# A layer of a hybrid streaming encoder on one core: its program is ordered by another timing model

## The chip, the core and the metric

The kernel runs on one core of a Trainium2 chip (trn2). The metric is the device time of one execution in microseconds (us), the median of several runs; less is better. The engines are called PE (TensorE, the matmuls), PEld (its weight loads), DVE (VectorE), ACT (ScalarE), POOL (GpSimd) and SP (SyncE, which here issues every DMA).

## The reference, cut to what matters

One layer is computed for a prompt of 2048 tokens and a sample of 32 tokens, all in float32, with model width 1024:

```python
def layer(x):                                   # for the prompt and for the sample
    z = rms_norm(x, norm1) @ w_in               # 3592 columns: 7 streams of 512, and 8 forget logits
    o_a = hgrn2(q, f, i)                        # 4 heads, state 128x128, chunks of 64 tokens, in order
    o_a = rms_norm_head(o_a) * silu(g)
    o_b = softmax(q k / 8 + sums of log f) v    # 8 heads of 64, causal, q and k RMS-normed
    x = x + concat(o_a, o_b) @ w_out
    return x + square(relu(rms_norm(x, norm2) @ w_up)) @ w_down     # 4096 hidden columns
```

Keys, values, forget logits and the recurrent states are outputs too.

## The kernel before, in words

**Tiling.** The prompt is cut into four quarters of 512 tokens, numbered 0 to 3; quarter 2 also carries the 32 tokens of the sample (544 columns, done as twice 272). Each float32 operand is split into a high and a low part in fp32r, and each product is made of three matmuls (`mm3`, lines 174 to 181, through the helper `mm`, line 100: high by high, high by low, low by high). So a tile of a projection, 1024 rows deep, is 24 matmuls of 128x128 by 512 columns that accumulate in one PSUM tile of the tag `mm`, of which there are two before the feed-forward part and three in it.

**Weights.** `load_w` (lines 158 to 171) brings a block of 512 KB through SP into `wr`, makes its high part on ACT (`wh`, line 163) and its low part on POOL in four instructions of 256 columns (`wl`, line 169). Each of the three has two buffers.

**POOL's other work.** The norms of rows (`build`, lines 222 to 264) add their sums and raise them to the power -0.5 on POOL (`rs`, lines 249, 155 and 156); DVE multiplies the row by that (`row`, line 251), PE transposes it (`ta`, line 104), and ACT and DVE make `ahi` and `alo` of it (lines 201 and 202). The norms along partitions (`squares`, lines 286 to 295) make a square and its low part on POOL (`t`, lines 290 and 294), which PE sums (`tk`, `tq`, `th`).

**Side work and main work.** The main work, called dense, is the projections: `fox` (the attention's streams), `heads` (the recurrent part's streams), `out_proj` and `ffn`. Beside it run generators of small steps: the recurrent part's tails (`xa`, `th`, `xu`, four times `xo`, with the state `S` on DVE, line 717), and the attention (`st`, `ot`, `mx`, `mt`, `rs`), whose PSUM tiles of the tag `x` are three in all. Small results of the tails live in twelve buffers of the tag `t`.

**What sets the order.** The program is written out by one Python function. The class `Flow` (lines 41 to 72) keeps a clock of its own that each matmul moves on by its estimated time; a side step that yields a latency is due that much later on this clock, and `dense` lets all due steps in after every three matmuls:

```python
    def dense(self, *gens):
        for g in gens:
            for _ in g:
                self.pump()
```

The latencies are constants (line 88: 5.0, 8.0, 7.0 and 4.5; line 90 paces the attention). What `Flow` writes is the program's order, and an instruction's place in it is its priority. After that the tile library's context plays the whole program on a timing model: whenever the model finds an engine free, the first instruction in priority whose inputs and buffers the model has ready is put next on that engine. The outcome is one fixed list for each engine and for SP's queue, with semaphore waits. On the chip each engine goes through its list in order and waits where the list is too early. The stages at the end of the function follow each other as

```python
    flow.dense(fox(A, (0,)))                       # quarter 0, then 1
    flow.dense(heads((0, 1), (0, 1)), heads((0,), (2, 3)))
    flow.dense(heads((1,), (2, 3)))                # then fox for 2 and 3, and heads((2, 3), ...)
    tmp_stack.close(); ps_stack.close()            # buffers of the first half end here
    flow.dense(out_proj(0), out_proj(1)); ffn(0); ffn(1) with out_proj(2); ffn(2) with out_proj(3); ffn(3)
```

(shortened; the last two lines stand in lines 1327 to 1361). `build(2)` writes the activations of quarter 2 over those of quarter 0, so it ends after the last projection of quarter 0, and `fox` of quarter 2 needs it.

Of the kernel before, what the change touches and what calls it, by code (L numbers as in the profile page):

```python
# [71 lines left out]
                self.pump()  # L72


@with_exitstack
def hymba_step(
    ctx: ExitStack,
    tc: tile.TileContext,
    x_prompt, x_sample, cache_k, cache_v, cache_logf, state_hgrn,
# [1316 lines left out]
```

## Time and profile before

| | |
|---|---|
| median of 3 runs | 2918.09 us (2916.07 to 2918.6) |
| profiled execution | 2912.88 us, of it 2911.2 us from the first to the last instruction |
| mean granted TensorE clock | 0.996 |
| busy: PE, PEld, DVE, ACT, POOL | 2847.8, 2423.8, 1680.2, 1386.3, 1278.7 us |

The busy time of an engine is the union of its instructions' records. The profiled execution is 5.2 us shorter than the median of the runs, and 1.7 us of it lie outside the span of instructions.

### The profile page before, as it was taken

Reading aid. Unit: us, or ns where it says so; the run is one execution under the profiler, and the core shown is the slowest. Engines: PE = TensorE matmul, PEld = TensorE weight load, DVE = VectorE, ACT = ScalarE, POOL = GpSimd, SP = SyncE. Lnnn points to the kernel's source line nnn. Section 1 sums busy time; section 2 is a strip of 40 time slices with the busy share of each in tenths; the row PEclk is TensorE's granted clock in tenths of the full one; section 3 lists DMA queues with packets and bytes.
Section 4 is the critical chain, followed back from the end, with each engine's and each line's share of the span. In section 5 each row is a group of like instructions: output and inputs, shape, how many; then the busy total and the mean of one; then the engine's idle time right before and its main releaser. Section 6 shows DMA issues by size and latency. Waiting matters only on the chain.

```text
span 2911.2 us, 43685 instructions
## 1 busy us (share of the span) xinstructions
PE 2847.8 (98%) x15568; PEld 2423.8 (83%) x15568; DVE 1680.2 (58%) x3283; ACT 1386.3 (48%) x2447; POOL 1278.7 (44%) x1744
## 2 busy tenths in 40 slices
PE   7999999999999999999999999999999999999999
PEld 5787877988789778888888888978999989988887
DVE  6336677656666677666565555465665554443333
ACT  5555676777555545444444444444444433222222
POOL 5653344453223444444444444434333454455554
PEclk9999999999999999999999999999999999999999
DMA  6762444776324563434347344444533333243333
GB/s 180 211 170 86 122 137 127 208 193 175 87 80 116 168 227 106 123 107 122 111 123 228 117 120 116 129 134 117 180 113 102 92 109 95 87 131 105 94 94 102
DMA packets 463658, 381.91 MB, mean 131 GB/s; under 512 B 34432, under 2 KB 363408, under 8 KB 463440
## 3 DMA queue, kind: packets, MB, share of 16 engines
q1 hardware_dynamic: 463440, 379.12, 44.9%
q8 instruction: 123, 2.02, 0.3%
q14 instruction: 95, 0.78, 0.1%
HBM read 316.63 MB, written 62.40 MB: 130 GB/s over the span
## 4 chain that ended last, share of the span: by engine, by line
PE 64%; DVE 1%; ACT 0%; DMA 0%; POOL 0%; issue 0%; SPq 0%; DVEq 0%; ACTq 0%; POOLq 0%
PE mm L100 55%; PE st L100 3%; PE ot L100 3%; PE mx L100 1%; PE ta L104 0%; DMA row<-X 0%; PE rs L100 0%; DMA acc<-in_x_prompt_dram 0%; PE tx L104 0%; PE ty L104 0%; POOL wl L169 0%; DVE acc L882 0%; PE mt L104 0%; DVE pl L878 0%; ACT wh L163 0%
## 5 line engine op out<-in xcount | busy, mean ns | idle before, releaser
L169 POOL TENSOR_TENSOR wl<-wr,wh 128x256 fp32r<-128x256 f32 x1536 | 1121.2, 761 | 1500.3 <-ACT wh L163 1354.6
L100 PE MATMUL mm<-ahi,wh 128*128 128x512 f32 (+1 forms) x2528 | 895.9, 354 | 2.4 <-DVE acc L1056 1.3
L100 PE MATMUL mm<-alo,wh 128*128 128x512 f32 (+1 forms) x2528 | 881.7, 349 | 0.0
L100 PE MATMUL mm<-ahi,wl 128*128 128x512 f32 (+1 forms) x2528 | 881.2, 349 | 0.0
L163 ACT CAST wh<-wr 128x1024 fp32r<-128x1024 f32 x384 | 403.3, 1050 | 749.5 <-PE mm L100 668.4
L100 PEld LDWEIGHTS mm<-ahi,wh 128*128 128x128 f32 x2528 | 478.2, 189 | 62.3 <-DVE t L628 1.7
L100 PEld LDWEIGHTS mm<-ahi,wl 128*128 128x128 f32 x2528 | 477.2, 189 | 59.2 <-issue 0.5
L100 PEld LDWEIGHTS mm<-alo,wh 128*128 128x128 f32 x2528 | 478.4, 189 | 56.3
L1056 DVE TENSOR_TENSOR acc<-acc,mm 128x512 f32<-128x512 f32 x480 | 326.5, 685 | 161.5 <-PE mm L100 159.0
L874 ACT ACTIVATE st<-st 128x512 f32<-128x512 f32 (+1 forms) x320 | 169.3, 529 | 332.9 <-PE st L100 189.0
L878 DVE TENSOR_TENSOR pl<-st,ph 128x512 fp32r<-128x512 f32 (+1 forms) x320 | 198.5, 620 | 204.3 <-ACT ph L876 203.3
L100 PE MATMUL mm<-wh,uh 128*128 128x512 f32 x768 | 306.9, 400 | 1.3 <-ACT uh L1117 0.8
L100 PE MATMUL mm<-wh,ul 128*128 128x512 f32 x768 | 302.9, 395 | 0.0
L100 PE MATMUL mm<-wl,uh 128*128 128x512 f32 x768 | 302.8, 394 | 0.0
L1116 DVE TENSOR_TENSOR mm<-mm,r 128x512 f32<-128x512 f32 (+1 forms) x160 | 95.9, 599 | 300.6 <-ACT r L1115 299.0
L100 PEld LDWEIGHTS mm<-wh,uh 128*128 128x128 f32 x768 | 144.6, 188 | 39.3 <-DVE acc L1056 5.5
L100 PEld LDWEIGHTS mm<-wh,ul 128*128 128x128 f32 x768 | 144.9, 189 | 35.0 <-DVE ul L1118 0.2
L882 DVE TENSOR_TENSOR acc<-acc,st 128x512 f32<-128x512 f32 (+2 forms) x288 | 173.5, 602 | 0.0
L876 ACT CAST ph<-st 128x512 fp32r<-128x512 f32 (+1 forms) x320 | 169.9, 532 | 7.4
L100 PEld LDWEIGHTS mm<-wl,uh 128*128 128x128 f32 x768 | 145.0, 189 | 30.8
L834 DVE TENSOR_REDUCE mc<-mx 128x1 f32<-128x512 f32 x192 | 130.6, 686 | 41.2 <-PE mx L100 40.6
L100 PE MATMUL mm<-uh,wh 128*128 128x272 f32 x512 | 149.5, 292 | 0.2 <-DVE acc L1149 0.2
(293 smaller groups left out, 4177.6 us busy)
## 6 DMA issues: line engine op xcount, KB each, us to landing
wr<-in_w_up_dram SPq DMA_DIRECT2D x128, 512.0 KB
wr<-in_w_down_dram SPq DMA_DIRECT2D x128, 512.0 KB
wr<-in_w_in_dram SPq DMA_DIRECT2D x96, 512.0 KB
kB<-KS SPq DMA_DIRECT2D x160, 128.0 KB
kA<-KS SPq DMA_DIRECT2D x80, 256.0 KB
V<-VS SPq DMA_DIRECT2D x80, 256.0 KB
wr<-in_w_out_dram SPq DMA_DIRECT2D x32, 512.0 KB
out_dram<-t SPq DMA_DIRECT2D x32, 256.0 KB
```

What stands on the lines that cost most here:

```text
L100: pe.matmul(out, lhsT, rhs, start=start, stop=stop)
L163: act.copy(hi, raw)
L169: pool.tensor_tensor(fl(lo)[:, s], fl(raw)[:, s], fl(hi.bitcast(F32))[:, s], op=ALU.subtract)
L834: dve.tensor_reduce(out=mc[:, j, kb:kb + 1], in_=mx[:, 0:n], axis=AX.X, op=ALU.max)
L874: act.activation(st[:, off:], st[:, off:], AF.Exp)
L876: act.copy(ph[:, off:], st[:, off:])
L878: dve.tensor_tensor(pl[:, off:], st[:, off:], ph.bitcast(F32)[:, off:], op=ALU.subtract)
L882: dve.tensor_tensor(acc[:, off:], acc[:, off:], st[:, off:], op=ALU.add)
L1056: dve.tensor_tensor(acc[:, t, c], acc[:, t, c], ps, op=ALU.add)
L1116: dve.tensor_tensor(z, z, r, op=ALU.mult)
```

## The change

The function is renamed `hymba_body` and keeps its text. A new `hymba_step` is called in its place. It opens a critical section of the outer context, in which the outer context doesn't order instructions, and inside it a second tile context on the same core, made with `schedule_with_timeline_sim=True`. The body is written into that second context, with the same `Flow`, constants, tiles and buffers. The second context orders it as described above, but plays it on the library's more detailed timing model (sequencers with queues of issued instructions, the tails of writes, the time a semaphore takes, the PE clock, fixed costs of POOL's instructions, which by the library's own description the plain model leaves out) in place of the plain one.

```diff
+def hymba_step(outer: tile.TileContext, *args):
+
+    with outer.tile_critical(), tile.TileContext(outer.nc, schedule_with_timeline_sim=True) as tc:
+        hymba_body(tc, *args)
+
+
 @with_exitstack
-def hymba_step(
+def hymba_body(
     ctx: ExitStack,
     tc: tile.TileContext,
     x_prompt, x_sample, cache_k, cache_v, cache_logf, state_hgrn,
```

## Rows read from the trace of the kernel before

**Rows 1.** The page's first part: busy time, share of the span and instructions

```profile
PE 2847.8 (98%) x15568; PEld 2423.8 (83%) x15568; DVE 1680.2 (58%) x3283; ACT 1386.3 (48%) x2447; POOL 1278.7 (44%) x1744
```

**Rows 2.** Busy time by stage: window, length, busy and count per engine, clock, DMA

```profile
0.00:25.00 25.00, 8.22 (x37) 5.93 (x38) 21.40 (x55) 15.87 (x36) 10.99 (x29) 1.00 0.74 206
25.00:200.00 175.00, 168.55 (x781) 135.11 (x779) 57.12 (x99) 100.81 (x180) 118.52 (x148) 0.98 0.71 195
200.00:430.00 230.00, 220.78 (x1272) 183.28 (x1271) 160.75 (x366) 145.05 (x270) 81.39 (x99) 1.00 0.40 112
430.00:520.00 90.00, 82.23 (x525) 71.07 (x526) 67.99 (x151) 60.65 (x131) 40.09 (x51) 0.96 0.50 145
520.00:660.00 140.00, 140.00 (x847) 123.62 (x846) 86.68 (x185) 99.71 (x202) 74.10 (x87) 1.00 0.71 196
660.00:1000.00 340.00, 332.01 (x2124) 281.98 (x2124) 227.16 (x506) 200.72 (x414) 110.28 (x128) 0.99 0.44 124
1000.00:1040.00 40.00, 36.46 (x163) 27.47 (x162) 31.04 (x61) 22.13 (x41) 10.38 (x14) 1.00 0.72 246
1040.00:1800.00 760.00, 758.68 (x3395) 621.43 (x3394) 473.65 (x822) 332.96 (x528) 334.44 (x477) 1.00 0.45 131
1800.00:1960.00 160.00, 155.17 (x886) 134.25 (x885) 88.95 (x154) 73.21 (x132) 65.90 (x99) 0.99 0.45 130
1960.00:2560.00 600.00, 599.32 (x4040) 560.45 (x4039) 333.24 (x691) 238.25 (x398) 261.30 (x374) 1.00 0.38 112
2560.00:2911.00 351.00, 346.35 (x1514) 279.22 (x1512) 132.18 (x203) 96.91 (x120) 171.35 (x243) 1.00 0.36 105
```

**Rows 3.** Timeline of PE around 991: start, length, instruction, idle and releaser

```profile
987.28 0.40 PE L100 MATMUL th<-t,oner 128*128 128x512 f32 x1
991.00 0.50 PE L100 MATMUL th<-t,oner 128*128 128x512 f32 x1 [3.32 <-POOL t L294]
991.34 0.40 PE L100 MATMUL mm<-ahi,wh 128*128 128x512 f32 x1
...
992.47 0.63 PE L100 MATMUL mm<-alo,wh 128*128 128x512 f32 x1
992.89 0.63 PE L100 MATMUL mm<-ahi,wl 128*128 128x512 f32 x1
```

**Rows 4.** Timeline of POOL before the same wait

```profile
986.55 3.18 POOL L169 TENSOR_TENSOR wl<-wr,wh 128x256 fp32r<-128x256 f32 x3
989.69 1.26 POOL L294 TENSOR_TENSOR t<-t,t 128x512 fp32r<-128x512 f32 x1
```

**Rows 5.** Timeline of PE, then DVE, then POOL, around 447

```profile
447.12 0.58 PE L104 MATMUL mt<-identr,mpad 128*2 128x128 f32 x4 [4.16 <-DVE t L756]
...
444.72 1.28 DVE L251 SCALAR_TENSOR_TENSOR row<-row,rs,gbc 128x1024 f32<-128x1024 f32 x1 [2.82 <-POOL rs L156]
...
440.80 2.83 POOL L169 TENSOR_TENSOR wl<-wr,wh 128x256 fp32r<-128x256 f32 x4 [5.18 <-ACT wh L163]
```

**Rows 6.** Who waited for whom, all engines: total us, times, longest

```profile
DVE row L251 <- POOL rs L156: 49.2, 17, 7.9
```

**Rows 7.** Chain that ended last, in order of time: start, us, what

```profile
1034.74 26.15 PE mm L100 x114
...
2335.39 56.97 PE mm L100 x297
```

**Rows 8.** Timeline of the start and of the end

```profile
0.78 1.28 ACT L142 ACT_TABLE_LOAD   x1 [0.78 <-PEq L1383]
...
2907.19 0.69 DVE L1056 TENSOR_TENSOR acc<-acc,mm 128x512 f32<-128x512 f32 x1 [0.71 <-PE mm L100]
```

**Rows 9.** SP's queue around the attention's end

```profile
2338.55 0.34 SPq L923 DMA_DIRECT2D MTH<-mh  x1
...
2341.81 0.37 SPq L274 DMA_DIRECT2D ahi<-MTH  x1
```

## The prediction

> **What bounds the kernel now.** I read the page's busy line first. PE is busy for 2847.8 of 2911.2 us, the next engine for 58% of the span [rows 1]. So no other engine's throughput matters, and a change of order alone can only act on what PE loses: the time in which it stands idle, and the time in which its clock is low. The table by stage says where that is [rows 2]. Idle time of PE is length less busy time: 16.8 us in the first 25, then 6.5, 9.2, 7.8, 0.0, 8.0 and 3.5 us in the stages up to 1040, 1.3 us from 1040 to 1800, 4.8 us from 1800 to 1960, 0.7 us from 1960 to 2560, and 4.7 us in the last stage: 63.2 us in all. The feed-forward part is closed. The 39.8 us of the stages 25 to 1040 and 1800 to 1960 are what an order could win, for there the small steps of the side work stand between the dense matmuls, and dense matmuls stand behind each wait.
>
> The timelines show what such a wait is. At 987.28 PE does the first of two sums over squares and then idles 3.32 us for POOL's `t`, although a dense matmul that waited for nothing comes right behind, at 991.34 [rows 3]. POOL was late because three pieces of a weight's low part, 3.18 us, lay before the 1.26 us that PE needed [rows 4]. The list had put the sum there because the model that made it had POOL done by then. At 447 it is the same one step removed: POOL does four pieces of a weight (2.83 us) before a row's `rs`, DVE's `row` waits 2.82 us for that, the DVE instructions behind it wait with it, one of them releases PE, and PE has lost 4.16 us [rows 5]. DVE waits for this `rs` 17 times, 49.2 us in total [rows 6]. These waits are errors about POOL's time, in lists that are otherwise good.
>
> After the wait at 991 the matmuls start 0.42 us apart (992.47, 992.89) [rows 3], where 114 matmuls of the same width in a closed stretch took 26.15 us, 0.229 each [rows 7]. That is the lower of the clock's two levels, 1.2 against 2.4 GHz, and PE had idled 3.3 us before it fell. By stage the granted clock is 0.98, 0.96, 0.99 and 0.99 in the stages from 25, 430, 660 and 1800 [rows 2]. At half speed half of the time is lost, so one minus the mean clock is the share lost: 175 x 0.02 + 90 x 0.04 + 340 x 0.01 + 160 x 0.01 = 12.1 us, with two digits of clock behind it.
>
> **The change part by part.** Instructions are neither added nor taken away in the body: the three matmuls of each product, POOL's pieces and every DMA stay, so the sum has no term for work.
>
> *A better place for waiting steps.* The detailed model has the fixed cost of POOL's instructions, semaphore times and write tails, so where it sees the sum over squares not ready it lets dense matmuls go first. All 39.8 us are the upper bound, nothing the lower one. A wait that goes away must find ready dense matmuls: at 991 and 447 they stood right behind. It does not find them where a stage has run out of dense work, as in parts of 430 to 520 (`build(2)` must end before `fox` of quarter 2) and 1000 to 1040 (the buffers of the first half end). And a model is not the chip: waits of 0.1 to 0.5 us will be made anew. I take half, -19.9 us. What is late next, when PE no longer waits for a sum, is that sum's own chain (`th`, the norm, the product with the gate, the DMA to DRAM), some us later; `out_proj` reads it much later, so it costs nothing outside the two stages just named.
>
> *The clock.* It falls after the long waits, not the short ones. Between 0 and 12.1 us come back; I take a third, -4.0 us, since half of the waits stay.
>
> *The section and the second context.* One more entry and exit are added around the body. The nearest rows are those of the one there is: ACT's first instruction stands 0.78 us after the start [rows 8], and 1.7 us of the profiled execution lie outside the span. A second set like these is 2.5 us. Below, nothing, if the outer one has nothing to wait for; above, the last store must land before the exit too: the last sum ends at 2907.9 and the span at 2911.2 [rows 8], so 3.3 us more, 5.8 us. Nothing hides this, because it lies before the first and after the last work. I take +2.0 us.
>
> The launch's own barriers have larger figures in the Trainium skill, "Runtime: NRT & Kernel Launch", section The ~15µs preamble/postamble breakdown: some 3.1 us before a kernel and 1.5 us after it. If a section cost such a pair, 4.6 us, the forecast would be 2898.8 us by the page in place of 2896.2 by the rows; no run so far shows which.
>
> *SP's queue, ACT and POOL.* The lists of these change too. In the feed-forward part a weight block takes POOL 2.8 us [rows 5] and serves 24 matmuls of 0.229 us, 5.5 us, so there is slack of a factor of two on POOL, and PE loses 2.0 us in the 1360 us from 1040 to 1800 and 1960 to 2560 [rows 2]. I cost these edits at nothing. The cover is the second buffer of `wr`, `wh` and `wl`; gone, each late block would cost PE its lateness.
>
> *The attention.* It may come later against the dense work. It ends at 2338.6 with its last DMA, and the load of that last quarter of `out_proj(3)`'s input follows at 2341.8 [rows 9], while PE goes on without a gap from 2335.4 for 57 us, most of it that `out_proj` [rows 7]. Three quarters of it don't need the late part, so a lateness up to some 40 us is hidden.
>
> Sum, on the profiled execution: 2912.9 - 19.9 - 4.0 + 2.0 = 2891.0 us. The median of the runs lies 5.2 us higher, so 2896.2 us is forecast, 0.75% under 2918.1. What a measurement of this kernel can tell from no change is about 0.2%, 6 us.
>
> **The rivals.**
>
> *Slower: chains stretched by run-ahead.* A detailed model has a sequencer that issues ahead of its engine. If the choice is made at issue, a step that becomes ready goes behind all matmuls already issued. How far this reaches the trace can't say; the two `mm` tiles bound it: one tile beyond the running one is 24 matmuls, 24 x 0.229 = 5.5 us, and nothing is the other end. A tail of the recurrent part visits PE nine times (`xa`, two `th`, `xu`, four `xo`, the sum), so it has eight such delays. Under dense work they cost nothing, but at 430 to 520 and 1000 to 1040 the dense work waits for the last tail. At half the bound each place costs 8 x 2.75 = 22 us, both 44 us; with half of the forecast's gain left, 12, and the section, 2: 2918.1 + 44 - 12 + 2 = 2952 us. It decides from a delay of 22 / 16 = 1.4 us per visit, where it eats the forecast's gain. For it: the side steps' latencies in `Flow` were set without such a delay, the four `xo` above all, and buffers of the tags `x` (three) and `t` (twelve) would be held longer. Against it: where dense work runs out nothing is issued ahead either, so the delay dies away just there.
>
> The Trainium skill, "TensorE: Matmul & The Clock Gate", gives PE an engine queue depth of 64 in the table at its head; as an estimate by that page, 32 pairs of load and matmul at 0.229 us would be 7.3 us of delay, above the turning point. No row of the trace shows that queue.
>
> *No change.* If almost every instruction is found ready in both models, the lists hardly differ, and only the section is added: 2920 us. For it: PE is 98% busy, so few places have a choice. Against it: the waits at 447 and 991 are errors in POOL's time, which the new model is said to know.
>
> *All of it.* All waits between 25 and 1040 and 1800 and 1960 go, and the clock with them: 2918.1 - 39.8 - 12.1 + 2.0 = 2868 us. Against it: the two stages without dense work.
>
> **How the numbers follow.** Forecast (2878 to 2911 us) 0.38; all of it 0.12; no change 0.17; chains stretched 0.25; slower for another reason (a weight block or a buffer late in the feed-forward part, some 10 to 60 us) 0.08. Faster by over 0.2%: 0.50, the same 0.17, slower 0.33. The range for 8 in 10 goes from 2866, the rival "all of it" at its bound, to 2956, just over the stretched chains; the forecast's own range stands above.
>
> **What would show it.** Right: waits of PE and DVE for POOL are shorter, the idle time of PE from 25 to 1040 falls from 35.0 us to about half of it, the stages after 1040 stay as they are, the mean clock rises above 0.996. The section: a gap of 1 to 3 us before the first DMA or after the last. The chains: `xo` and `xa` further apart, PE idle around 430 to 520 and 1000 to 1040 grown by tens of us. Wrong altogether: a new wait of PE for weights in the feed-forward part, which would be a case that I cost at nothing.

## The result, and the profile after

The changed kernel takes 2991.14 us (median, 2990.13 to 2995.31) against 2918.09: the ratio is 1.0258, with a 95% interval of 1.0245 to 1.0272. The forecast was 2896, with a range up to 2956. The time went the other way, and past the range.

The page's first part, after. The instructions are those of [rows 1]; PE's busy time is 38.7 us longer, in a span that is 78.4 us longer (2989.6 us).

```profile
PE 2886.5 (97%) x15568; PEld 2442.1 (82%) x15568; DVE 1668.2 (56%) x3283; ACT 1376.9 (46%) x2447; POOL 1277.1 (43%) x1744
```

Busy time by stage after, columns as in [rows 2].

```profile
0.00:25.00 25.00, 4.82 (x19) 3.62 (x20) 19.82 (x52) 13.90 (x32) 13.91 (x32) 1.00 0.73 206
25.00:200.00 175.00, 158.12 (x707) 123.98 (x706) 56.25 (x106) 88.40 (x161) 100.59 (x127) 0.95 0.63 171
200.00:430.00 230.00, 218.87 (x1191) 180.01 (x1190) 140.23 (x303) 131.92 (x242) 82.59 (x96) 0.99 0.38 108
430.00:520.00 90.00, 82.27 (x470) 67.41 (x469) 67.71 (x153) 58.32 (x124) 35.85 (x49) 0.94 0.43 129
...
660.00:1000.00 340.00, 319.15 (x1871) 264.19 (x1872) 201.99 (x455) 186.91 (x388) 100.31 (x118) 0.94 0.41 115
...
1800.00:1960.00 160.00, 160.00 (x879) 139.53 (x878) 78.40 (x146) 63.93 (x106) 67.06 (x95) 1.00 0.42 124
```

PE's idle time is 2989.6 - 2886.5 = 103.1 us, 39.9 more than before. It grew where the side work runs: 16.8 to 20.2 us in the first 25, 6.5 to 16.9 up to 200, 8.0 to 20.9 from 660 to 1000. The clock column fell with it: 0.98 to 0.95, 0.96 to 0.94, 0.99 to 0.94. By stage these and the 0.99 from 200 to 430 make 175 x 0.05 + 230 x 0.01 + 90 x 0.06 + 340 x 0.06 = 36.9 us, 25 more than the 12.1 of before; by the mean clocks of the whole span, 0.986 and 0.996, it is 41.9 against 11.6 us, 30 more. So idle time and clock make some 65 to 70 of the 78.4 us; what makes the rest of PE's longer busy time is open. From 1800 to 1960 the 4.8 us that PE idled are gone.

Where the loss ends is seen in one tile. These are the instructions of `xo`, the last steps of the tails: first of before, then after; count, shortest/median/longest in ns, first and last start in us, and below who waited for them or for ACT's copy of them.

```profile
L100 PE MATMUL xo<-AT,t x128: 274/275/276, 234.8 to 1007.6; 128*128 128x128 f32 x128
...
  POOL t L290: 23.8, 8
...
  ACT t L724: 4.5, 4
```

```profile
L106 PE MATMUL xo<-AT,t x128: 275/275/421, 258.1 to 1091.4; 128*128 128x128 f32 x128
...
  POOL t L296: 46.5, 9
  ACT t L730: 18.4, 10
```

The last `xo` comes 83.8 us later, and what is left of the span behind it is shorter: 2989.6 - 1091.4 = 1898.2 us against 2911.2 - 1007.6 = 1903.6. All of the loss lies ahead of the feed-forward part, and ACT now waits 18.4 us for `xo` and POOL 46.5 us for ACT's copy of it, four times and twice as long.

Who PE waits for has changed too. The view of waits after: total us, times, longest.

```profile
DVE row L257 <- POOL rs L162: 21.8, 11, 5.2
...
PE mx L106 <- DMA qC<-QS: 10.5, 6, 3.7
...
PE ot L106 <- ACT ph L882: 7.9, 9, 2.3
...
PE mm L106 <- DVE t L634: 6.8, 4, 3.3
...
PE mm L106 <- ACT t L423: 4.6, 3, 3.7
...
PE th L106 <- POOL t L300: 1.8, 1, 1.8
```

The waits that the prediction spoke of did shrink: DVE's for `rs` from 49.2 [rows 6] to 21.8 us, and no sum over squares waits 3.3 us for POOL any more. But over all rows of this view PE's own waits for POOL go only from 4.1 to 3.4 us and those for DVE stay at 52, while those for ACT go from 2.3 to 28.5 us and those for DMAs from none to 11.1. These two make 37 of the 39.9 us.

What such a place looks like. PE's timeline before at the sample's steps, and after at the same steps:

```profile
774.59 0.75 PE L100 MATMUL th<-t,oner 128*128 128x512 f32 x4
775.19 0.48 PE L100 MATMUL st<-qC,kB 98*128 98x512 f32 x1
775.51 0.40 PE L100 MATMUL st<-qA,kA 128*128 128x512 f32 x1
775.75 0.40 PE L100 MATMUL mm<-ahi,wh 128*128 128x512 f32 x1
...
778.75 0.39 PE L100 MATMUL mm<-alo,wh 128*128 128x512 f32 x1
778.98 0.38 PE L104 MATMUL ts<-identr,kc 128*64 128x128 f32 x2
```

```profile
834.42 0.29 PE L106 MATMUL mm<-alo,wh 128*128 128x272 f32 x1
834.54 0.29 PE L106 MATMUL mm<-ahi,wl 128*128 128x272 f32 x1
...
836.18 0.39 PE L106 MATMUL st<-qA,kA 128*128 128x512 f32 x1
836.57 0.40 PE L106 MATMUL th<-t,oner 128*128 128x32 f32 x2
839.09 0.80 PE L106 MATMUL ot<-ph,V 128*128 128x512 f32 x1 [2.13 <-ACT ph L882]
839.69 0.63 PE L110 MATMUL ts<-identr,kc 128*64 128x128 f32 x2
...
843.70 0.63 PE L106 MATMUL st<-qA,kA 128*128 128x512 f32 x1
...
844.98 0.43 PE L106 MATMUL mm<-ahi,wh 128*128 128x272 f32 x1
845.21 0.43 PE L106 MATMUL mm<-alo,wh 128*128 128x272 f32 x1
```

Before, 14 dense matmuls stand between `st` and the next side step, and ACT makes `ph` under them. After, `ot` follows its `st` with nothing between but a small sum: PE idles 2.13 us for ACT, and ten microseconds of side steps follow each other (834.7 to 845.0). Behind that the matmuls of 272 columns start 0.23 us apart; ahead of the bunch it was 0.12 (834.42 and 834.54). That is the lower of the clock's two levels: the granted clock is 1.00 from 800 to 838.5 us, 0.51 from 838.6 to 848.8 and 1.00 again behind that. It fell while PE idled, behind 2.3 us of side steps (834.67 to 836.96) with nothing dense between them.

### The profile page after: what moved, and what is told of

It reads as the page before. It is cut to its first block, busy times and chain, and to the rows that moved or that the text cites. A ratio compares the mean times of both kernels' runs of the same rounds, so it can differ in the third digit from the quotient of the medians.

```text
span 2989.6 us, 43716 instructions
## 1 busy us (share of the span) xinstructions
PE 2886.5 (97%) x15568; PEld 2442.1 (82%) x15568; DVE 1668.2 (56%) x3283; ACT 1376.9 (46%) x2447; POOL 1277.1 (43%) x1744
## 4 chain that ended last, share of the span: by engine, by line
PE 87%; DVE 5%; ACT 3%; DMA 2%; issue 2%; POOL 0%; SPq 0%; ACTq 0%; DVEq 0%; POOLq 0%
PE mm L106 72%; PE st L106 4%; PE ot L106 4%; PE mx L106 2%; PE xo L106 1%; DMA qC<-QS 1%; PE ta L110 1%; DMA row<-in_x_prompt_dram 1%; PE xa L106 1%; ACT wh L169 1%; PE xu L106 1%; PE th L110 0%; PE rs L106 0%; DVE pl L884 0%; DVE mm L1122 0%
## 5 line engine op out<-in xcount | busy, mean ns | idle before, releaser
L106 PE MATMUL mm<-wh,uh 128*128 128x512 f32 x768 | 298.8, 398 | 3.6 <-DVE ul L1124 2.4
```

The costliest lines, as they stand in the source:

```text
L106: pe.matmul(out, lhsT, rhs, start=start, stop=stop)
```

## The experiments

Three theories: **one**, PE's list is at fault, by steps that come late or by steps bunched together; **two**, the lists of ACT, DVE and POOL are at fault; **three**, the section costs. Each set of runs has its own median of before; they lie between 2915.8 and 2917.1 us.

**Section and model apart.**

```diff
-    with outer.tile_critical(), tile.TileContext(outer.nc, schedule_with_timeline_sim=True) as tc:
+    with outer.tile_critical(), tile.TileContext(outer.nc, schedule_with_timeline_sim=False) as tc:
```

> The changed kernel with the second context's option set back to the plain model: the critical section and the second context stay. If the lists of the detailed model cost the 73 us, this stands within 6 us of the kernel before (2916 to 2924 us), the section itself being worth 0 to 3 us. If the section costs (for instance by SP's DMA issues, whose median is 0.60 us in the changed kernel and 0.42 us before), it stands near the changed kernel, 2970 us or more, with DMA issues of 0.6 us.

Measured: 2921.76 us, ratio 1.0017 (1.0007 to 1.0026).

```diff
-    with _tile.TileContext(nc) as tc:                                    # the kernel before
+    with _tile.TileContext(nc, schedule_with_timeline_sim=True) as tc:
         hymba_step(tc, *args)
```

> The kernel before with the detailed model as the option of its one context, without section or second context. If the lists cost, within 10 us of the changed kernel (2980 to 3000 us). If the section costs, near the kernel before, 2910 to 2925 us. DMA issues of 0.4 us would show that their length comes with the section, 0.6 us that it does not.

Measured: 2985.20 us, 1.0239 (1.0224 to 1.0254). The model costs some 68 us and the section some 5 (4.7 by the first run; 5.9 between this run and the changed kernel, which were not measured in one set). Theory three falls as the main cause. But longer DMA issues come with the section: an issue of a weight block on SP takes, shortest/median/longest, with the section and the plain model

```profile
L167 SPq DMA_DIRECT2D wr<-in_w_up_dram x128: 601/616/666, 1125.0 to 2883.6; - x128
```

and with the detailed model and no section

```profile
L161 SPq DMA_DIRECT2D wr<-in_w_up_dram x128: 367/368/479, 1203.2 to 2947.8; - x128
```

**PE's list or the others'.** Two runs hold engines to the program's order inside the context with the detailed model; a third holds PE alone to it with the plain one, by the helper shown further down:

```diff
+    with tc.manual_schedule(engines={EngineType.PE}):                    # or the other four engines
         hymba_step(tc, *args)
```

> Detailed model, no section, but PE's list is held to the program's order, while ACT, DVE, POOL and SP are ordered by the model. Theory one, PE's list is at fault (side steps stand some 20 to 40 matmuls behind their place, attention steps before dense matmuls): back to 2910 to 2930 us. Theory two, the lists of ACT, DVE and POOL are at fault by themselves: it stays at 2960 us or more.

> Detailed model, no section, the lists of ACT, DVE, POOL and SP held to the program's order, PE's list left to the model. Theory one (PE's list): still slow, 2960 us or more. Theory two (the other lists): back to 2910 to 2930 us.

> Plain model, PE's list held to the program's order: the control for the run with the detailed model and PE so held (3007 us). If it stands near 2917 us, the 90 us there came from the other engines' lists; if it stands at 2985 us or more, they came from holding PE to the program's order, whatever the model, and that run says nothing on the other lists.

Measured: 3007.41 us, 4479.51 us and 2999.96 us. The third shows that the first told nothing of the theories: holding PE to the program's order costs 83 us with the plain model already, and 90 with the detailed one. Counted in the lists, the plain model moves only 795 of PE's 15136 instructions to a later place than the program has (and 611 to an earlier one), and these moves are worth 83 us. The second says as little: the program's order of the other four engines is no list to run at all.

The better way is to hold PE to a list that one model made, and let the other model choose the rest. A helper at the end of the body writes the order down (shortened: the unpacking of `code` is left out):

```diff
+def pin_order(tc, engine, code):                # code: how far each place is from the program's
+    mine = [i for i in tc.nc.cur_bb.bb.instructions if i.engine == engine]
+    line = [mine[k + d] for k, d in enumerate(decode(code))]
+    for before, ins in zip(line, line[1:]):
+        tc.add_manual_dep(ins, before.name, DependencyInfo(NoSync, DATA), reason="written order")
     flow.until(lambda: not flow.q)
+    pin_order(tc, PE, ORDER_PE)
```

> One context, no section, plain model, but PE's list is held to the very list that the detailed model made (as in the second run of the first set); the lists of ACT, DVE, POOL and SP are the plain model's choice around it. Theory one (PE's list is at fault): within 15 us of 2985, so 2970 to 3000 us. Theory two (the lists of the other engines are at fault): 2915 to 2935 us.

> The other way round: detailed model, with PE's list held to that of the kernel before; the lists of ACT, DVE, POOL and SP are the detailed model's choice around it. Theory one: 2910 to 2930 us. Theory two: 2960 us or more. Both by half: 2940 to 2960 us.

Measured: 3045.57 us, 1.0440 (1.0424 to 1.0455), and 2939.62 us, 1.0078 (1.0063 to 1.0093). Against the set's 2916.9 for both plain and 2985.2 for both detailed, PE's list costs 129 us with the other lists chosen by the plain model around it, the other lists cost 23 us around the plain model's PE list, and both together 68. Neither run came where one of the theories put it: the first lies 45 us above its range, the second just under "both by half". Where the first run loses is seen in the last `xo`; here are the first run and the second:

```profile
L100 PE MATMUL xo<-AT,t x128: 274/275/422, 255.1 to 1101.6; 128*128 128x128 f32 x128
L100 PE MATMUL xo<-AT,t x128: 275/275/276, 238.1 to 1028.6; 128*128 128x128 f32 x128
```

Before, the last `xo` starts at 1007.6 us, and with all lists detailed and no section at 1086.6. Up to there PE's list costs 94 us, the other lists 21, and both 79. Behind it the first run takes 1941.3 us to the end of its span where before takes 1903.6: 38 us that neither model's own set of lists loses. A mixed set has losses of its own, here by loads that come late, the longest

```profile
PE ot L100 <- DMA V<-VS: 9.8, 1, 9.8
```

Theory one is the main cause; theory two holds for the smaller part. The lists of one model fit each other: of the 60 us between 129 and 68, the detailed lists of ACT, DVE, POOL and SP take 15 from the damage of PE's list ahead of the last `xo`, and 45 lie behind it.

**Where.** The lists of PE, ACT, DVE and SP are held up to one time only (shortened):

```diff
+    for e in (PE, ACT, DVE, SP):
+        pin_order(tc, e, FIRST[e])              # a prefix; the rest of e stands behind it
```

> Detailed model, one context, but the lists of PE, ACT, DVE and SP up to what ran by 1140 us in the kernel before are held to those of the kernel before; behind that the detailed model chooses. If all of the loss lies ahead of the feed-forward part: 2905 to 2920 us, and near 2912 if the detailed model takes away the 4.8 us that PE idles from 1800 to 1960. If the feed-forward part loses too: 2930 us or more.

> The other half alone: plain model, one context, the lists of PE, ACT, DVE and SP up to the same point (1225 us in the run with the detailed model and no section) held to the detailed model's, behind that the plain model chooses. If all of the loss lies ahead of the feed-forward part: 2985 to 3000 us.

Measured: 2913.49 us, 0.9993 (0.9984 to 1.0003), and 2989.25 us, 1.0254 (1.0238 to 1.0269). All of the loss is made ahead of the feed-forward part, and the first run, as fast as before, shows that holding lists to a written order costs nothing by itself. Behind it the detailed model does what was hoped for at one place, the wait at 1926; the row of the first run there is

```profile
1800.00:1960.00 160.00, 159.47 (x911) 138.49 (x910) 76.99 (x134) 66.94 (x118) 74.77 (x108) 1.00 0.44 130
```

0.5 us idle against 4.8 [rows 2]. In the whole that gain is not clear of the measurement.

**Late steps or bunched steps.** These are the two branches of theory one; the expectations here call lateness one and bunching two. Both are in the detailed model's PE list. Counted in dense matmuls ahead of a step, `xo` stands 33 later than in the plain list, `xu` 28, `xa` 21, `th` 18 (means), while the attention's `ot` stands, up to 1230 us, some 11 earlier in the mean and at the same place in the median. By time, from the end of the record that made a step's last input to the step's start, before and after, in the mean over the 16 tails: the first matmul of `xa` that reads `qx` 5.1 and 8.8 us, the first of `xu` 0.7 and 3.0, all of `xo` 3.7 and 5.5, but `ot` (160 to 1230 us) 6.4 and 3.4. The runs write these one at a time into the plain list, from place 650 to 4500, which is 164 to 883 us of before; the loss of the changed kernel goes on to the last `xo`. The edit is another written list each time; the rules by which it was made, in words:

```text
late(k):   a side step is put out when k further dense matmuls have been put out (24, 12; -6: earlier)
bunch:     side steps are collected, and put out when 16 are there or the oldest is 12 late
```

> Plain model, one context. PE's list is that of the kernel before, but from its place 650 to 4500 every step of the side work stands 24 dense matmuls (one tile, 5.5 us at 0.229 us each) later; no step is put together with others. In the detailed model's list the tails' steps stand later by 33 dense matmuls (xo, mean), 28 (xu), 21 (xa) and 18 (th). Theory one, lateness of the tails stretches the chain: 40 us or more on top of 2917, so 2957 us or more. Theory two, steps bunched together without dense matmuls between them: less than 15 us on top, 2932 us at most.

> As the run with all side steps 24 dense matmuls later (2976 us, 60 us on top), with 12. If the cost grows with the lateness from the first matmul on: 2940 to 2955 us. If the places have slack for 2.7 us and only more than that costs: 2917 to 2930 us.

> The same stretch of PE's list with every side step 6 dense matmuls earlier. If PE then waits for inputs that are not ready (the tight places that the detailed model's list has for attention steps, 3.5 us behind their input in place of 6.4, would cost by themselves): 2935 us or more. If the places have slack on this side: 2910 to 2925 us.

> Plain model, one context. PE's list is that of the kernel before, but from its place 650 to 4500 the steps of the side work are collected and let out when 16 are there or the oldest has waited for 12 dense matmuls: 505 of 1379 steps then stand in runs of 16 or more (32 of 1379 in the kernel before, 421 of 1384 in the detailed model's list), and a step is 5.7 dense matmuls later in the mean. Theory two, bunching: 2945 us or more. Theory one, lateness: a quarter of what 24 dense matmuls cost, at most 2930 us.

Measured: 24 later 2976.43 us, 1.0212 (1.0196 to 1.0227); 12 later 2924.83, 1.0028 (1.0018 to 1.0037); 6 earlier 2936.20, 1.0065 (1.0051 to 1.0079); bunched 2959.21, 1.0150 (1.0135 to 1.0165). Lateness costs, but not from the first matmul on: 12 matmuls, 2.7 us a visit, cost 8.5 us, and 24 cost 60. Earlier costs as well, 20 us for 6. Of the shifts that were run, to both sides, none is better than the places that the latencies in `Flow` and the plain model give. Bunching costs 43 us with steps 5.7 matmuls later in the mean, where 12 without bunching cost 8.5: it is a cost of its own. So neither branch of theory one can be left out; how the 94 us divide between them is not shown, for the detailed list moves its steps unevenly and no run took one branch out of it. The largest wait that 24 brought is one that before does not have; PE's waits in that run:

```profile
PE mm L100 <- ACT t L476: 14.8, 6, 4.1
```

Dense matmuls wait for ACT to empty a PSUM tile into a buffer `t`. That the late steps hold the twelve buffers of that tag too long is argued, not shown: more of them were not tried.

**Could the waits be had away at all?** In PE's list of before, the step that waits, with the side steps behind it, is put behind as many dense matmuls as the wait was long, and two more. The rule by which the list was written, in words:

```text
if wait[step] > 3.0:                        # 99.8, 447, 991, 1926 us; > 1.0: 13 places
    hold(step, ceil(wait[step] / 0.229) + 2)
```

> Plain model, one context. PE's list is that of the kernel before, but at its four long waits (at 99.8, 447, 991 and 1926 us, 16.0 us together) the step that waits, with the side steps behind it in order, stands 18 to 21 dense matmuls later. If a wait that goes away is won, as the prediction took for granted: 16 us of waits and, with the lower clock behind them (12 us by stage, most of it behind these four), up to 24 us: 2893 to 2903 us. If the wait only comes back at the next step, which depends on the moved one: within 6 us of 2917.

> The same for all 13 waits of side steps over 1 us (28.9 us together). If waits that go away are won: 2882 to 2898 us, 5 us or more under the run with four. If moved steps make new waits behind them: no better than the run with four, or slower than before.

Measured: 2909.01 us, 0.9972 (0.9960 to 0.9983), and 2910.70, 0.9980 (0.9971 to 0.9989). Of up to 24 us 7.3 are won with four, and nothing more with 13. PE's timeline of the run with four says which:

```profile
448.26 0.43 PE L104 MATMUL ta<-identr,row 32*128 32x32 f32 x4 [4.04 <-DVE alo L202]
...
985.92 0.39 PE L100 MATMUL th<-t,oner 128*128 128x512 f32 x1
...
1920.41 0.79 PE L100 MATMUL mm<-wh,uh 128*128 128x512 f32 x1 [5.37 <-DVE ul L1118]
```

The sum at 991 (now 986) waits for nothing, and the one at 99.8 is gone but for 2 us. At 447 a wait of 4.0 us is back at a next step. It is not for the late `row` any more, which comes 3.9 us sooner than before [rows 5]; it ends with DVE's `alo`, behind DVE's other work:

```profile
440.82 1.28 DVE L251 SCALAR_TENSOR_TENSOR row<-row,rs,gbc 128x1024 f32<-128x1024 f32 x1 [2.83 <-POOL rs L156]
...
447.93 0.28 DVE L202 TENSOR_TENSOR alo<-ta,ahi 128x128 fp32r<-128x128 f32 x1
```

At 1926 a dense matmul now waits 5.4 us for DVE's `ul`, which stands on DVE behind a `row` that waits for POOL's `rs`:

```profile
1916.08 1.27 DVE L251 SCALAR_TENSOR_TENSOR row<-row,rs,gbc 32x1024 f32<-32x1024 f32 x1 [5.86 <-POOL rs L156]
...
1919.68 0.67 DVE L1118 TENSOR_TENSOR ul<-mm,uh 128x512 fp32r<-128x512 f32 x1
```

Two of the four waits went, and two came back at another step that DVE releases.

**Both gains in one kernel.** The list of the run with four waits up to 1132 us, the detailed model behind it:

> One context. The lists of PE, ACT, DVE and SP up to 1132 us are held to those of the run with the four moved waits; behind that the detailed model chooses. If the gains add up: that run's 7 us, its lost 1.5 us at 1920 us back, and the 4 to 5 us that the detailed model's list saves from 1800 to 1960: 2902 to 2906 us. If the detailed model's choice is worth nothing there: 2908 to 2911 us.

Measured: 2905.18 us, 0.9966 (0.9952 to 0.9980). That is in the range of gains that add up. Its median is 3.8 us under that of the run with four waits, but the intervals of the two overlap, so the sum is not shown clear of the measurement; PE's idle time from 1800 to 1960 is 0.5 us in place of that run's 6.3. It is the fastest kernel here, 0.34% under the kernel before.

**What makes the section cost.**

```diff
+    with _tile.TileContext(nc): pass            # first run: a second context, no section
     with _tile.TileContext(nc) as tc:
+        with tc.block():                        # second run: a block, no section
             hymba_step(tc, *args)
```

> The kernel before with an empty context opened and closed ahead of its own, no critical section, plain model. If a second context makes DMA issues longer: a weight block's issue takes 0.6 us and the time is 2919 to 2925 us. If the critical section does: 0.37 us, and 2915 to 2920 us.

> The kernel before with its body in a block of its one context, no critical section, plain model. If a block of its own makes DMA issues longer: 0.6 us and 2919 to 2925 us. If the critical section does: 0.37 us, and 2915 to 2920 us.

Measured: 0.9999 (0.9990 to 1.0009) and 1.0003 (0.9994 to 1.0012), with issues of a weight block at 0.373 us in both. Neither makes SP's DMA issues longer. What is left is the critical section, by itself or with a context inside it; it was not run without one.

## Why the prediction was wrong, point by point

**What bounds the kernel**: right. PE stayed at 97% busy, and most of the time moved by PE's idle time (39.9 us) and its clock (25 us by stage, 30 by the mean clocks).

***A better place for waiting steps***, -19.9 us: this is the step that failed. It took the lists as good but for some waits, so that the change could only act on these, with nothing as its lower bound. The detailed model gave four in five of PE's 15136 instructions another place, and these places made new waits: PE's list alone brings the last `xo` 94 us later. Moved in the plain list, side steps 24 dense matmuls later cost 60 us, 6 earlier 20, and bunched 43. The half that it took for won is also too much: with only these moved in PE's list, four waits of 16.0 us, worth up to 24 with the clock, gave 7.3 us. Its parts were right in kind: the waits for POOL shrank, and the wait at 1926 went.

**The clock**, -4.0 us: wrong in sign, as a consequence. It falls not only behind long waits, as was said: at 838.6 it fell inside 2.13 us of idling that followed a run of side steps. Before shows it already: the granted clock is 0.54 from 824.5 to 827.9 us, and the longest wait ahead of that, at 822.98, is 1.91 us.

**The section**, +2.0 us, 0 to 5.8: right in kind, sized too small. It is 4.7 us by the run with the section alone (2.0 to 7.6 by its interval). The exit is part of it, as was said: in that run's last rows

```profile
2914.22 0.69 DVE L1062 TENSOR_TENSOR acc<-acc,mm 128x512 f32<-128x512 f32 x1 [0.71 <-PE mm L106]
```

the last sum ends 4.3 us before the end of the span (2919.3), where it was 3.3 us [rows 8]. At the start the first DMA is issued 0.2 us later and PE's first projection matmul comes at 24.1 us in place of 22.3. Not in the working were DMA issues of 0.61 in place of 0.37 us; that they make the rest of the late start, by SP's first loads, is argued, not shown.

**SP's queue, ACT and POOL**, cost at nothing: wrong ahead of 1040, right behind it. The detailed lists of these engines cost 23 us around the plain model's PE list. One place is the start: ACT's list has the sums of `row` ahead of `ahi`, from which DVE makes the `alo` that PE waits for, and ACT waits there for a DMA. ACT's timeline after, and PE's:

```profile
13.57 0.56 ACT L207 CAST ahi<-ta 128x512 fp32r<-128x512 f32 x1
16.67 0.63 ACT L252 ACTIVATE junk<-row 128x512 bf16<-128x512 f32 x1 [2.54 <-DMA row<-in_x_prompt_dram]
...
17.30 0.57 ACT L207 CAST ahi<-ta 128x512 fp32r<-128x512 f32 x1
...
24.38 1.97 PE L110 MATMUL ta<-identr,stage 128*128 128x128 f32 x8 [4.62 <-DVE alo L208]
```

PE's first projection matmul comes at 28.8 us in place of 22.3, and at 27.2 in the run that has the plain model's PE list and no section: 5 of the 23 us are lost there.

**The attention**, hidden up to some 40 us: it lost nothing by ending late, for its last `ot` starts at 2324.5 us where it was 2330.1. What the prediction did not price is that its steps come closer behind their inputs: `ot` waits 7.9 us for `ph` and 5.4 for `pl`, before none and 0.9. What this costs by itself was not run.

**The rival of the stretched chains**, 0.25, 2952 us: right that the tails' steps come later, wrong in the path by which that costs. The delay per visit that it took, 2.75 us, lies among what the trace has (3.7 for `xa`, 2.3 for `xu`, 1.7 for `xo`). Its turning point was 1.4 us a visit, where the run with 2.7 us costs 8.5 us. It priced two stages, in which dense work waits for the last tail, at 44 us. But PE idles as long from 430 to 520 as before (7.7 and 7.8 us), and where the last tails now run

```profile
1040.00:1130.00 90.00, 80.96 (x399) 61.45 (x398) 59.98 (x118) 47.51 (x86) 29.14 (x36) 0.96 0.62 199
```

it idles 9.0 us in place of 3.5; the loss lies all along the side work. Bunching, which came with the lateness, was not in it. The prediction's estimate by the Trainium skill, "TensorE: Matmul & The Clock Gate", the table at its head, was 7.3 us for a queue of 64. Of the tails' steps only `xo` stands that far back in the list, 33 matmuls or 7.6 us at 0.229 each; `xu`, `xa` and `th` stand 6.4, 4.8 and 4.1 us back. No run here shows the chip's own queue, and that the lateness comes from a queue in the model is not shown.

**No change** and **all of it** are out: four in five of PE's instructions have another place, and the time went the other way.

## What to carry to other kernels

Where two planners' lists are to be compared, hold one engine to the one list and let the other planner place the rest: two kernels tell which list is at fault. Read them only up to where the loss is made, for a mixed set of lists has losses of its own (38 us here). Before counting waits as winnings, ask what else stands on the late engine: of four waits moved here two came back at another step. A model with more parts can make the worse list. That it did so here because the program's latencies were set with the other model is argued, not shown: no run set them anew for the detailed one. Shifting the places of a stretch to both sides shows how much slack they have.

## What the runs showed of the hardware that was not expected

With the body in a critical section SP takes 0.61 us to issue a 512 KB load where it takes 0.37 us without one, with the same instruction, all through the program: the median over all 1462 issues is 0.60 us against 0.42. A second context ahead of it or a block does not do it; whether the section does it by itself or only with a context inside it is open, and so is the reason.
